# The second FFN of a diffusion layer on one Trainium2 core: where its first loads stand in the queue, where its operand forms are computed, and when a block's last turns are issued

## The chip, the cores and the metric

The kernel runs on one core of one Trainium2 chip. The metric is the time of one execution on the device in microseconds (us). The kernel before took 2631.93 us in the median of 3 runs (2630.71 to 2635.68). The profile shows one more execution of it.

## What is computed

The reference is one layer of a diffusion backbone: a half-step SwiGLU FFN on 256 context tokens and 256 latent tokens, a token mixer (attention heads and mLSTM heads), and a second half-step SwiGLU FFN on the latent tokens alone, all in fp32. The change touches only the second FFN:

```python
def adaln(x, g, mod, i):
    return rms_norm(x, g) * (1 + mod[:, i + 1, None, :]) + mod[:, i, None, :]

def half_step_ffn(x, mod, i, g, w_up, w_down):
    h = adaln(x, g, mod, i)
    a, b = jnp.split(h @ w_up, 2, axis=-1)
    return x + 0.5 * mod[:, i + 2, None, :] * ((jax.nn.silu(a) * b) @ w_down)

    ...
    xl = half_step_ffn(xl, mod_l, 6, g_norm[l, 2], w_ffn2_up[l], w_ffn2_down[l])
    ...
    return rms_norm(xl, g_final)
```

Here x is 256 x 2048, w_up is 2048 x 11264 (two halves, a and b, of 5632 columns) and w_down is 5632 x 2048.

## The kernel before

**Split products.** Every fp32 factor is split into a high part, rounded to the matmul's input type (`hi`, ScalarE, line 123), and the remainder (`lo`, VectorE, line 124). One product is three matmuls, hi by hi, hi by lo, lo by hi (lines 145 to 147). A weight tile is 128 x 2048 fp32, 1 MB, and is split in two halves of 1024 columns. The halves go into a pool of four `hi` and four `lo` buffers, so the split of a half waits until TensorE has used up the half four places before it. Weights that are used as they come land in `raw`, a pool of three buffers; the next load into a buffer waits for the `lo` of the tile that it held.

**Blocks of columns.** The 5632 columns of the hidden layer are 11 blocks (numbers 0 to 10) of 512. Block 0 is worked out while the layer norm is still unfinished (`products`, `tail`); its last quarter (the two loads `in_w_up`, line 138) runs until the change's first place. Block 1 is the *plain block*: `up(1)` has eight steps, one 1 MB tile each and 24 matmuls of 128x512. Blocks 2 to 10 (`QUADS`) go through `quad(n)`, a scheme of seven half-size products in the manner of Strassen: 14 steps of one 1 MB tile and 12 matmuls each, into two PSUM accumulators X and Y. The left factors are quarters of h (`a11`, `a12`, `a22`) and four combinations of them, the *forms* `n1`, `s2`, `s4` and `s3`, each again as a high and a low part. They are computed once, by `token_forms`, with VectorE and ScalarE instructions. The right factors are combinations of weight tiles, and these are formed in SBUF: a tile of the *chain* is loaded, split, and then another weight tile is added to it by an accumulating DMA that GpSimd (POOL) issues (`accum`, line 726). There are two sets of two such tiles, `chain2c` and `chain2r`, and they change roles from block to block.

**The order of the work.** The program text sets it, and the tile framework then orders the instructions of each engine by its own estimate. First come three steps of `up(1)`, each followed by a step of `token_forms`; then quad 2 with the other five steps of `up(1)` and the first of `down0` between its steps; from then on each quad has four steps of the down product (24 matmuls each) between its 14 steps. Each engine takes its instructions in order, and so does the queue of SP, which issues most loads: an issue that waits for its buffer holds up all issues behind it.

**The two places of the change.** At the first, after block 0, the pools of the layer norm are closed and three things are put on the right side of SBUF in their place: the accumulator of the output `acc2` (128 x 2 x 2048), the four chain tiles and the forms. The first loads of the four chain tiles stand right behind this in the program (lines 1985 to 1988). `token_forms` takes one buffer of the `raw` pool for its two temporaries, from its first step until `s3` has been written, which waits for the sixth tile of `up(1)`. At the second place, the end of each quad, `c21` works out the second half of the gated values (`ca`, 128 tokens x 512 columns), and its *turn* is entered in a list: four 128x128 transposes on TensorE (line 2053) and two instructions that put the result into the hidden tiles `hid2h` and `hid2l`. A turn is issued when the clock that counts the steps has reached its entry; that of `c21` is entered with 2 steps to go.

## Time and profile before

| | |
|---|---|
| median of 3 runs | 2631.93 us |
| the profiled execution | 2630.98 us, its span 2629.3 us |
| TensorE busy | 2580.3 us, 98% of the span |
| VectorE busy | 2181.8 us, 83% |
| ScalarE busy | 1446.4 us, 55% |
| mean granted TensorE clock | 0.993 |
| second FFN from the plain block on | 1950.5 us to the end |

The page of the profile gives busy times over the whole span; the stage of the change is its last quarter. In the rows that follow, PE is TensorE, DVE is VectorE, ACT is ScalarE, SPq is SP's queue of DMA issues. A row of the timeline has the start, the duration, engine, line, operation, output and inputs by the program's names, the shape and the count; in square brackets stands how long the engine had been idle and what ended that. A row of the waits has the waiting engine and line, what it waited for, the sum in us, the number of waits and the longest.

### The profile page before, as it was taken

What the parts mean: (1) busy time and instruction counts of PE and PEld (TensorE: products, weight loads), DVE (VectorE), ACT (ScalarE), POOL (GpSimd) and SP (SyncE); (2) the same over time, 40 slices, a digit from 0 to 9 for tenths busy, and PEclk for the clock granted to TensorE, in tenths of its full rate; (3) what the DMA queues carried; (4) which work ended last, traced back from release to release, by engine and by line L of the source; (5) the groups of instructions that cost most, each with busy time, mean ns of one, the idle gap of its engine ahead of it and who ended that gap; (6) DMA issues with size and microseconds to landing.
All of it is one profiled execution on the core that took longest, in us unless ns stands there. A gap on an engine that the chain in (4) does not pass through costs nothing. (4 is left out here: it accounts for less than half of the span.)

```text
span 2629.3 us, 33786 instructions
## 1 busy us (share of the span) xinstructions
PE 2580.3 (98%) x12646; PEld 2141.9 (81%) x12646; DVE 2181.8 (83%) x2842; ACT 1446.4 (55%) x1862; POOL 221.2 (8%) x275
## 2 busy tenths in 40 slices
PE   8999999999999999999999999999989999999998
PEld 5788888888888878888889889878887877887787
DVE  7788888878888778888886889788987888888888
ACT  4454544454444465444454467566565766666664
POOL 0000010100010100000110000120000000000001
PEclk8999999999999999999999999999999999999999
DMA  9989999999999988889986877677667889999996
GB/s 390 356 211 267 282 267 283 253 271 283 278 268 282 262 238 235 226 217 231 230 236 267 313 260 260 229 252 283 235 233 208 262 257 266 268 269 260 268 273 196
DMA packets 127795, 685.20 MB, mean 261 GB/s; under 512 B 14216, under 2 KB 16776, under 8 KB 65040
## 3 DMA queue, kind: packets, MB, share of 16 engines
q1 hardware_dynamic: 98256, 491.15, 49.8%
q0 software_dynamic: 29376, 191.90, 37.0%
q8 instruction: 99, 1.62, 0.2%
q14 instruction: 64, 0.52, 0.1%
HBM read 665.11 MB, written 17.89 MB: 260 GB/s over the span
## 5 line engine op out<-in xcount | busy, mean ns | idle before, releaser
L123 ACT ACTIVATE hi<-raw 128x1024 fp32r<-128x1024 f32 (+2 forms) x488 | 504.3, 1040 | 410.3 <-PE mm L147 255.0
L124 DVE TENSOR_TENSOR lo<-raw,hi 128x1024 fp32r<-128x1024 f32 (+2 forms) x476 | 569.7, 1209 | 159.6 <-ACT hi L123 139.6
L145 PE MATMUL mm<-hi,hhi 128*128 128x512 f32 (+3 forms) x1024 | 393.8, 385 | 0.0
L146 PE MATMUL mm<-lo,hhi 128*128 128x512 f32 (+3 forms) x1024 | 386.9, 378 | 0.0
L147 PE MATMUL mm<-hi,hlo 128*128 128x512 f32 (+3 forms) x1024 | 386.9, 378 | 0.0
L123 ACT ACTIVATE hi<-chain 128x1024 fp32r<-128x1024 f32 x240 | 253.1, 1059 | 239.4 <-PE mm L147 131.8
L124 DVE TENSOR_TENSOR lo<-chain,hi 128x1024 fp32r<-128x1024 f32 x240 | 290.2, 1222 | 77.3 <-ACT hi L123 76.0
L203 DVE SCALAR_TENSOR_TENSOR junk<-sraw,cBh 128x1024 fp8e5<-128x1024 f32 x192 | 234.5, 1221 | 25.4 <-DMA sraw<-in_w_mt 23.1
L147 PEld LDWEIGHTS mm<-hi,hlo 128*128 128x128 f32 x1024 | 192.5, 188 | 33.8
L145 PEld LDWEIGHTS mm<-hi,hhi 128*128 128x128 f32 x1024 | 192.6, 188 | 31.1
L146 PEld LDWEIGHTS mm<-lo,hhi 128*128 128x128 f32 x1024 | 192.8, 188 | 30.6
L124 DVE TENSOR_TENSOR lo<-chain2c,hi 128x1024 fp32r<-128x1024 f32 x112 | 135.5, 1223 | 43.5 <-ACT hi L123 39.4
L123 ACT ACTIVATE hi<-chain2c 128x1024 fp32r<-128x1024 f32 x112 | 117.0, 1058 | 81.6 <-PE mm L147 40.0
L124 DVE TENSOR_TENSOR lo<-chain2r,hi 128x1024 fp32r<-128x1024 f32 x104 | 125.9, 1223 | 41.0 <-ACT hi L123 37.2
L123 ACT ACTIVATE hi<-chain2r 128x1024 fp32r<-128x1024 f32 x104 | 108.8, 1058 | 71.1 <-PE mm L147 30.7
L146 PE MATMUL mm<-lo,hid2h 128*128 128x512 f32 x352 | 137.4, 391 | 0.7 <-DVE lo L124 0.7
L147 PE MATMUL mm<-hi,hid2l 128*128 128x512 f32 x352 | 136.9, 389 | 0.0
L145 PE MATMUL mm<-hi,hid2h 128*128 128x512 f32 x352 | 135.8, 389 | 0.0
L203 DVE SCALAR_TENSOR_TENSOR sr<-sr,cBl 128x1024 f32<-128x1024 f32 x85 | 102.6, 1218 | 15.2 <-DMA sr<-in_w_mt 15.0
L726 POOL DMA_DIRECT2D chain<-in_w_up1b x60 | 53.0, 884 | 723.9 <-DVE lo L124 697.0
L145 PE MATMUL mm<-hhi,hi 128*128 128x512 f32 (+1 forms) x288 | 101.2, 351 | 0.0
L146 PE MATMUL mm<-hlo,hi 128*128 128x512 f32 (+1 forms) x288 | 98.9, 343 | 0.0
(513 smaller groups left out, 5848.7 us busy)
## 6 DMA issues: line engine op xcount, KB each, us to landing
raw<-in_w_dn SPq DMA_DIRECT2D x70, 1024.0 KB, 9.7
chain<-in_w_up1b POOLq DMA_DIRECT2D x60, 1024.0 KB, 10.8
sraw<-in_w_mt SPq DMA_DIRECT2D x96, 512.0 KB, 8.5
sr<-in_w_mt SPq DMA_DIRECT2D x82, 512.0 KB, 5.2
raw<-in_w_up1b SPq DMA_DIRECT2D x40, 1024.0 KB, 8.2
mraw<-in_w_m SPq DMA_DIRECT2D x32, 1024.0 KB, 7.5
chain<-in_w_dn POOLq DMA_DIRECT2D x30, 1024.0 KB, 8.5
chain2c<-in_w_up2b POOLq DMA_DIRECT2D x28, 1024.0 KB, 12.3
```

Of the source, the lines that this page charges most:

```text
L123: scalar[0].activation(hi, src, AF.Copy)
L124: vector[0].tensor_tensor(lo, src, hi.bitcast(F32), op=ALU.subtract)
L145: tensor[0].matmul(out_ap, sh, mh, start=first, stop=False, skip_group_check=skip)
L146: tensor[0].matmul(out_ap, sh, ml, start=False, stop=False, skip_group_check=skip)
L147: tensor[0].matmul(out_ap, sl, mh, start=False, stop=last, skip_group_check=skip)
L203: ins = nc.vector.scalar_tensor_tensor(junk() if junk else raw, raw, 1.0, cB[s], op0=ALU.mult, op1=ALU.mult, accum_out=mT[:, i, s, kt, h : ...
L726: accum = lambda dst, src: nc.gpsimd.dma_start(dst, src, accum_op=ALU.add)
```

## The change

The change has four parts, all in the second FFN.

1. The first loads of the chain tiles move in the program: those of `chain2c` behind the second step of the plain block (the load of its second tile), those of `chain2r` behind step 1 of quad 2.
2. The two temporaries of `token_forms` are no longer a `raw` buffer but columns 1024 to 2047 of `acc2`; the gate's values of the plain block (`sab`) stand in columns 0 to 511 of `acc2`. `down0` writes these columns later.
3. The turn of `c21` is entered with 4 steps to go in place of 2.
4. `sab` of block 0 moves to a pool that is closed after block 0, and the last block's temporary takes a `ca` buffer.

```diff
         def sab_tile():
-            return f2.tile([P, CB], F32, tag="sab", name="sab")
+            return scratch[-1].tile([P, CB], F32, tag="sab", name="sab", bufs=2)
...
-        for q in range(2):
-            nc.sync.dma_start(sets[0][q], part(QUADS[0], 0, q))
-        for q in range(2):
-            nc.sync.dma_start(sets[1][q], part(QUADS[0], 1, 2 + q))
+        def first_tiles(ab, c, tiles):
+            for q in range(2):
+                nc.sync.dma_start(tiles[q], part(QUADS[0], ab, c + q))
...
-            raw = raw_tile()
-            vs = [raw[:, x * 1024 : (x + 1) * 1024].rearrange("p (k c) -> p k c", k=8) for x in range(2)]
+            vs = [acc2[:, x, 1024:].rearrange("p (k c) -> p k c", k=8) for x in range(2)]
...
                 mul(g["a"], g["a"], g["y"])
-                turn.append((clock[0] + 2, n, 1, g["a"], -1.0))
+                turn.append((clock[0] + 4, n, 1, g["a"], -1.0))
...
-                                sab.append(sab_tile())
+                                sab.append(acc2[:, t, :CB])
...
-        for _ in range(3):
+        for n in range(3):
             unit()
+            if n == 1:
+                first_tiles(0, 0, sets[0])
             steps(forms)
         for n in QUADS:
...
                 clock[0] += 1
                 turned()
+                if n == QUADS[0] and step == 1:
+                    first_tiles(1, 2, sets[1])
                 if step % 2:
...
-                    y = sab_tile()
+                    y = ca_tile()
```

What this makes of the order, at three places. First the queue of SP, from the last quarter of block 0 (`in_w_up`) on; `raw<-in_w_up2b` of line 138 are the tiles of the plain block, those of line 2121 (now 2119) the first tiles of quad 2 that are used as they come. Before:

```order
L138 DMA raw<-in_w_up 128x2048 x2
L138 DMA raw<-in_w_up2b 128x2048
L1986 DMA chain2c_16100<-in_w_up2b 128x2048
L1986 DMA chain2c_16101<-in_w_up2b 128x2048
L1988 DMA chain2r_16102<-in_w_up2b 128x2048
L1988 DMA chain2r_16103<-in_w_up2b 128x2048
L138 DMA raw<-in_w_up2b 128x2048 x4
L2121 DMA raw<-in_w_up2b 128x2048 x2
```

And with the change:

```order
L138 DMA raw<-in_w_up 128x2048 x2
L138 DMA raw<-in_w_up2b 128x2048 x3
L1987 DMA chain2c_16100<-in_w_up2b 128x2048
L1987 DMA chain2c_16101<-in_w_up2b 128x2048
L1987 DMA chain2r_16102<-in_w_up2b 128x2048
L1987 DMA chain2r_16103<-in_w_up2b 128x2048
L138 DMA raw<-in_w_up2b 128x2048 x2
L2119 DMA raw<-in_w_up2b 128x2048 x2
```

Two tiles of the plain block now stand ahead of the four chain tiles.

Second, VectorE where block 0 ends and the forms begin; `raw` on the left of an arrow is the temporary of the forms, `lo<-raw,hi` is the split of a weight tile. Before:

```order
L1935 TENSOR_TENSOR hid2l<-sab,hid2h 128x256
L2013 TENSOR_TENSOR raw<-raw,h2lo 128x1024
L1999 TENSOR_TENSOR raw<-h2hi 128x1024
L1999 TENSOR_TENSOR raw<-raw,h2lo 128x1024
L2013 TENSOR_TENSOR raw<-raw,h2lo 128x1024
L1999 TENSOR_TENSOR n1f<-raw,n1f 128x1024
L1999 TENSOR_TENSOR raw<-raw,h2lo 128x1024
L2000 SCALAR_TENSOR_TENSOR raw<-raw,h2hi 128x1024
L1999 TENSOR_TENSOR raw<-raw,h2lo 128x1024
L1999 TENSOR_TENSOR s2f<-raw,s2f 128x1024
L2000 SCALAR_TENSOR_TENSOR raw<-raw,h2hi 128x1024
L124 TENSOR_TENSOR lo<-raw,hi 128x1024 x4
```

And with the change, where the temporary is `acc`:

```order
L1935 TENSOR_TENSOR hid2l<-sab,hid2h 128x256
L2011 TENSOR_TENSOR acc_16099<-acc_16099,h2lo 128x1024
L124 TENSOR_TENSOR lo<-raw,hi 128x1024
L1998 TENSOR_TENSOR acc_16099<-acc_16099,h2lo 128x1024
L124 TENSOR_TENSOR lo<-raw,hi 128x1024
L1998 TENSOR_TENSOR acc_16099<-h2hi 128x1024
L1998 TENSOR_TENSOR n1f<-acc_16099,n1f 128x1024
L124 TENSOR_TENSOR lo<-raw,hi 128x1024
L1999 SCALAR_TENSOR_TENSOR acc_16099<-acc_16099,h2hi 128x1024
L124 TENSOR_TENSOR lo<-chain2c_16100,hi 128x1024
L1998 TENSOR_TENSOR acc_16099<-acc_16099,h2lo 128x1024
L124 TENSOR_TENSOR lo<-chain2c_16100,hi 128x1024
```

The instructions of the forms no longer stand in one run ahead of four splits; a split stands behind each one or two of them. One more split (of the second plain tile) stands a few rows higher.

Third, TensorE at the start of a quad, where the turn of the quad before it stands (`tr<-ident,ca`). X is the first product, Y the second. Before, ahead of the last three matmuls of X:

```order
L146 MATMUL X<-lo,h2hi 128x512
L147 MATMUL X<-hi,h2lo 128x512
L2053 MATMUL tr<-ident,ca 128x128 x4
L145 MATMUL X<-hi,h2hi 128x512
L146 MATMUL X<-lo,h2hi 128x512
L147 MATMUL X<-hi,h2lo 128x512
L145 MATMUL Y<-hi,h2hi 128x512
```

And with the change, behind the twelfth of the 24 matmuls of Y:

```order
L145 MATMUL Y<-hi,h2hi 128x512
L146 MATMUL Y<-lo,h2hi 128x512
L147 MATMUL Y<-hi,h2lo 128x512
L2051 MATMUL tr<-ident,ca 128x128 x4
L145 MATMUL Y<-hi,h2hi 128x512
L146 MATMUL Y<-lo,h2hi 128x512
```

In quads 4 to 10 the turn moves back by 15 matmuls; the two instructions that take its result move with it, on both engines behind three more splits.

## The prediction

> **What bounds the kernel now.** First the page, for the engine that is busy longest:

> ```profile
> span 2629.3 us, 33786 instructions
> PE 2580.3 (98%) x12646; PEld 2141.9 (81%) x12646; DVE 2181.8 (83%) x2842; ACT 1446.4 (55%) x1862; POOL 221.2 (8%) x275
> ```

> TensorE (PE) is busy 98% of the span and the change takes no matmul away. So it can win only where TensorE stands idle, or runs at a lower granted clock, in the second FFN. The table by stages, from the plain block on, shows where that is (stretch, length, busy time and count of TensorE, its weight loads, VectorE, ScalarE and GpSimd, granted clock, DMA share, GB/s):

> ```profile
> 1950.70:1956.10 5.40, 5.40 (x24) 4.13 (x22) 5.34 (x7) 0.43 (x2) 0.00 (x0) 1.00 1.02 431
> 1956.10:1971.40 15.30, 5.91 (x15) 4.21 (x15) 13.93 (x12) 5.96 (x7) 0.00 (x0) 0.67 0.54 218
> 2001.20:2008.80 7.60, 5.06 (x15) 3.73 (x15) 5.73 (x6) 4.60 (x6) 0.00 (x0) 0.78 0.64 233
> 2124.40:2132.40 8.00, 6.28 (x20) 4.47 (x19) 5.78 (x6) 5.04 (x6) 0.14 (x1) 0.79 0.85 330
> 2132.40:2570.40 438.00, 430.12 (x1905) 350.79 (x1904) 377.14 (x350) 291.59 (x308) 36.45 (x42) 1.00 0.91 264
> ```

> Two holes lie in the plain block: A (15.3 us, 5.91 busy, clock 0.67) and B (7.6 us, 5.06 busy, clock 0.78). A third lies at the end of quad 3, and the 438 us behind it lose 7.9. TensorE's timeline has the idle times of A and B in brackets, between the first matmul of the plain block and the first of `n1` (product 3 of quad 2):

> ```profile
> 1950.49 0.40 PE L145 MATMUL mm<-hi,h2hi 128*128 128x512 f32 x1
> 1950.72 0.40 PE L146 MATMUL mm<-lo,h2hi 128*128 128x512 f32 x1
> ...
> 1964.02 1.22 PE L145 MATMUL mm<-hi,h2hi 128*128 128x512 f32 x2 [7.91 <-ACT hi L123]
> 1966.73 0.80 PE L146 MATMUL mm<-lo,h2hi 128*128 128x512 f32 x1 [1.49 <-DVE lo L124]
> ...
> 2003.06 0.50 PE L145 MATMUL mm<-hi,h2hi 128*128 128x512 f32 x1 [1.78 <-ACT hi L123]
> 2004.32 0.50 PE L146 MATMUL mm<-lo,h2hi 128*128 128x512 f32 x1 [0.76 <-DVE lo L124]
> ...
> 2011.30 0.39 PE L145 MATMUL Y<-hi,n1f 128*128 128x512 f32 x1
> ```

> Both end with a split. What the splits waited for stands on ScalarE, VectorE and SP's queue:

> ```profile
> 1945.58 0.80 SPq L1986 DMA_DIRECT2D chain2c<-in_w_up2b  x2
> 1947.60 0.92 SPq L138 DMA_DIRECT2D raw<-in_w_up2b  x2
> 1951.10 1.22 DVE L1999 TENSOR_TENSOR raw<-h2hi 128x1024 f32<-128x1024 f32 x1
> 1961.97 1.06 ACT L2006 ACTIVATE s2f<-raw 128x1024 fp32r<-128x1024 f32 x1 [4.82 <-DVE raw L1999]
> 1962.93 1.04 ACT L123 ACTIVATE hi<-raw 128x1024 fp32r<-128x1024 f32 x1
> 1997.10 2.60 SPq L138 DMA_DIRECT2D raw<-in_w_up2b  x2
> 2001.95 1.06 ACT L123 ACTIVATE hi<-raw 128x1024 fp32r<-128x1024 f32 x1 [4.24 <-DMA raw<-in_w_up2b]
> 2012.37 1.23 DVE L1999 TENSOR_TENSOR h2lo<-raw,h2hi 128x1024 fp32r<-128x1024 f32 x1 [0.64 <-ACT h2hi L2006]
> ```

> Hole A: plain tiles 2 and 3 are issued at 1947.60, behind the four chain tiles, and ScalarE takes tile 2 only at 1962.93, behind the copy of `s2` for which it had stood 4.82 us. Hole B: the load for the sixth plain tile is issued at 1997.10 and waited for; one of three `raw` buffers is the forms' until 2012.37, so two carry the stream.

> The waits of SP (1925 to 1990) and TensorE (2009 to 2580), by sum, count and longest:

> ```profile
> SPq L1986 <- DVE sab L1946: 12.0, 1, 12.0
> ...
> PE tr L2053 <- DVE ca L2071: 4.6, 6, 0.8
> PE Y L146 <- DVE lo L124: 2.9, 4, 0.8
> PE Y L145 <- ACT hi L123: 1.2, 2, 1.0
> ```

> SP stood 12.0 us, to 1945.58, before the first chain tile's issue, with the plain tiles behind it. And six times TensorE waits 0.8 us at the turn of `c21` for its product on VectorE (`ca`, L2071).

> **What the holes cost.** Idle: 7.91 + 1.49 + 1.78 + 0.76 = 11.9 us. Half clock: in A, (1 - 0.67) x 15.3 = 5.05 us lost at half rate means 10.1 us at it; idle were 1.49 and, from 1961 to 1964, some 3.2 of these, so 5.4 us of work cost 2.7 more; in B (1 - 0.78) x 7.6 = 1.7. Sum 16.3. End to end: 192 matmuls (six plain tiles of 24, four quad steps of 12) from 1950.49 to 2011.30 at 0.23 us, the step of the first two rows, are 44.2 of 60.8 us: 16.6 lost. I take 16.5.

> The idle 2.54 us of B was followed by a lower clock, so was 1.73 us at quad 3 (0.97 + 0.76), but not 1.04 us at quad 7:

> ```profile
> 2126.64 0.51 PE L145 MATMUL Y<-hi,h2hi 128*128 128x512 f32 x1 [0.97 <-ACT hi L123]
> 2127.90 0.67 PE L146 MATMUL Y<-lo,h2hi 128*128 128x512 f32 x1 [0.76 <-DVE lo L124]
> ...
> 2378.43 0.49 PE L145 MATMUL Y<-hi,h2hi 128*128 128x512 f32 x1 [0.28 <-ACT hi L123]
> 2379.69 0.50 PE L146 MATMUL Y<-lo,h2hi 128*128 128x512 f32 x1 [0.76 <-DVE lo L124]
> ...
> 2376.00:2384.00 8.00, 6.88 (x28) 4.86 (x27) 5.59 (x6) 5.96 (x6) 0.00 (x0) 1.00 0.96 375
> ```

> [...]

> **The change, part by part.**

> *The queue of SP.* Ahead of the chain tiles only buffers bind. The second and third plain tile take those of block 0's last two tiles, whose `lo` end at the first two rows:

> ```profile
> 1937.42 1.23 DVE L124 TENSOR_TENSOR lo<-raw,hi 128x1024 fp32r<-128x1024 f32 x1
> 1942.16 1.22 DVE L124 TENSOR_TENSOR lo<-raw,hi 128x1024 fp32r<-128x1024 f32 x1
> 1965.46 4.62 DVE L124 TENSOR_TENSOR lo<-raw,hi 128x1024 fp32r<-128x1024 f32 x4
> ...
> raw<-in_w_up2b SPq DMA_DIRECT2D x26, 1024.0 KB, 6.7
> ```

> So they are issued at 1938.7 and 1943.4 and land, at the median of 6.7 us, at 1945.4 and 1950.1. TensorE needs them at 1950.49 + 24 x 0.23 = 1956.0 and at 1961.5: covered by 10.6 and 11.4 us. The chain tiles are still issued at 1945.58, since their release (L1946) does not move; four tiles of 1.05 MB at the 431 GB/s of the first row are there by 1955.8, needed at 1967: covered by 11 us. The one POOL queue (accumulations) is fed by the chain's splits and moves forward with them.

> *The forms in `acc2`.* Three buffers carry the plain tiles all along. Tile 4 goes out behind the chain tiles and is needed at 1972.6; the sixth, late in B, goes out once tile 5 is split, near 1978, and is needed near 1990 (1972.6 + 72 matmuls). Hole B closes. Whether `acc2` waits for what lay under it the trace does not show: between 0 and the 12.0 us that SP waited for the neighbouring tiles. I take 0, because that wait ended at 1945.58 and the first form starts at 1951.10. VectorE is what is left: by the order it has 11 form instructions and 8 splits between the last `sab` (1951.1) and the split of the fourth plain tile, 19 x 1.14 us (the run of four in 4.62 us: 1.13 from start to start, 1.22 the last) and 0.34 for `hid2l`: done at 1973.1, needed at 1950.49 + 96 x 0.23 + 0.23 = 1972.8. I leave 0.5 us idle; bounds 0 and 3.1 (1.4 us idle, the middle of 1.04 and 1.73, and half clock behind it, 1.7).

> *The turn, 15 matmuls later.* 15 x 0.23 = 3.4 us covers the 0.8 us six times, 4.6 in all. But the next wait is close. At `n1` the chain tile's accumulation lands late; the rows of quads 5 and 8:

> ```profile
> 2211.85 2.01 ACT L123 ACTIVATE hi<-chain2r 128x1024 fp32r<-128x1024 f32 x2 [2.78 <-DMA chain2r<-in_w_up2b]
> 2218.58 1.22 DVE L124 TENSOR_TENSOR lo<-raw,hi 128x1024 fp32r<-128x1024 f32 x1
> 2220.02 0.39 PE L146 MATMUL mm<-lo,hid2h 128*128 128x512 f32 x1
> ...
> 2401.14 1.06 ACT L123 ACTIVATE hi<-chain2c 128x1024 fp32r<-128x1024 f32 x1 [3.72 <-DMA chain2c<-in_w_up2b]
> 2409.13 0.50 PE L146 MATMUL mm<-lo,hid2h 128*128 128x512 f32 x1 [0.33 <-DVE lo L124]
> ```

> From landing to TensorE runs an unbroken chain of `hi`, three `lo`, one tile addition (2.29 us) and one more `lo`. It hangs on the landing, not on the turn. In quad 5 it ends at 2218.58 + 1.22 = 2219.80, 0.2 us ahead of the matmul that reads it (2220.02); in quad 8 TensorE already waits 0.33. So of the 0.8 us won at a turn, 0.2 stay in a quad like 5 and nothing in one like 8: the wait only moves. I take 0.2 for quads 5, 6, 9 and 10 and 0 for 7 and 8, 0.8 together, and keep 0 and 4.6 as bounds.

> *Pools.* `sab` and `y` change addresses only; the `ca` buffers that `y` takes were last read by quad 10's turns, three down steps earlier. Nothing.

> **Sum.** 2630.98 - 16.5 + 0.5 - 0.8 = 2614.2 us for the profiled execution. The median of the runs is 0.95 above that execution: 2615.1.

> **Rivals.**

> *VectorE keeps a part of hole A (0.10).* If a split waits for a buffer just as a form is ready, the in-order chain slips; 3 us of slip and its half clock give 2615.1 + 2.5 + 1.7 = 2619.3. For: VectorE is full from 1951 to 1973, its slack 0.3 us. Against: every split in my count finds its `hi` by then.

> *DMA gives it back (0.06).* TensorE would be 16 us ahead and quads 3 and 4 wait for weights instead: if the hole at quad 3 grows by 13 to 16 us, 2628 to 2631. For: DMA share 0.91 over the quads. Against: 0.54 and 0.64 in A and B; the loads move forward too. [...]

> *Slower: half clock in every quad (0.04).* TensorE comes 0.8 us earlier to the tile that quad's last product takes, and the loads of the down product, earlier too, share the DMA engines with the accumulation into it. Today that wait (the rows of L145 and L146 on Y) is 1.73 us in quad 3, 1.04 in quad 7 and 1.3 in all the other quads together (2.9 + 1.2 less these two). If the accumulations land over 1.5 us later, it passes the point between 1.04 and 1.73 us in each of quads 4 to 10: 7 x (1.7 idle + 1.7 for half clock) = 23.8, less the 2.4 that stand there today, less 16 won: 2632 + 5 = 2637. For: quad 3 shows it once, DMA share 0.91. Against: the accumulation starts from a split that TensorE paces itself, behind the turn, so it moves with TensorE.

> *The change does not reach the queue:* excluded, since SP's order shows both tiles ahead.

> **How the numbers follow.** Forecast 0.80, VectorE 0.10, DMA 0.06, slower 0.04. Low end: no residue, all 4.6 us of the turns, and the 1.73 us idle at quad 3 gone by a new phase: 2615.1 - 0.5 - 3.8 - 1.7 = 2609.1; with a part of its half clock gone too, 2608. High end: residue 3.1, nothing from the turns, half clock once more: 2615.1 + 2.6 + 0.8 + 1.7 = 2620.2; with the VectorE rival's 2619 inside I close at 2620.5. About 0.2% (5.3 us) is what a measurement of this kernel tells from no change: faster 0.90, same 0.06, slower 0.04.

> **What would show it.** Right: TensorE without a break from 1950.5 to the first `n1` matmul, now near 1995, clock 1.00 throughout; plain tile 2 issued near 1938.7; no wait at the turn, and 0.5 to 1.1 us of new wait at `n1` in each quad from 5 on. Wrong: an idle time over 1.4 us near 1971 to 1976, a hole at quad 3 that has grown by several us, or half clock in the quads.

## The result, and the profile after

The changed kernel took 2615.26 us in the median of 4 runs (2613.28 to 2618.03), the kernel before 2631.32 us beside it (4 runs, 2629.84 to 2635.68): a ratio of 0.9937, with a 95% interval of 0.9919 to 0.9956. In a second set of runs the same kernel gave 0.9942 (0.9925 to 0.9960). The forecast was 2615.1 us, range 2608 to 2620.5. The profiled execution took 2613.28 us, 17.70 less than that of before.

The head of the page after:

```profile
span 2611.5 us, 33782 instructions
PE 2577.5 (99%) x12646; PEld 2139.1 (82%) x12646; DVE 2179.6 (83%) x2842; ACT 1445.9 (55%) x1862; POOL 221.5 (8%) x275
```

The table by stages of the changed kernel (same columns as before): the plain block's start, the stretch where hole A was, that of hole B 17 us earlier than before, the end of quad 3, and the 438 us behind it:

```profile
1940.00:1956.10 16.10, 16.10 (x115) 15.18 (x115) 14.12 (x19) 9.34 (x14) 0.00 (x0) 1.00 0.88 347
1956.10:1971.40 15.30, 15.30 (x70) 12.65 (x69) 15.30 (x15) 9.38 (x10) 0.96 (x1) 1.00 0.89 301
1984.20:1994.30 10.10, 10.10 (x47) 8.35 (x46) 9.48 (x9) 6.46 (x8) 0.00 (x0) 1.00 0.77 300
2107.40:2115.40 8.00, 8.00 (x37) 6.61 (x36) 7.87 (x9) 6.79 (x7) 1.70 (x2) 1.00 1.03 403
2115.40:2553.40 438.00, 430.36 (x1891) 347.89 (x1890) 373.36 (x347) 286.47 (x305) 34.87 (x41) 1.00 0.91 263
```

TensorE is busy in every microsecond of the first four stretches and the clock is 1.00 in all of them: A and B are gone, and so is the hole at quad 3, on which only the low end of the forecast's range had counted. VectorE is full in the second (15.30 of 15.30) and TensorE does not wait for it, by a narrow margin. The split of the fourth plain tile and the matmuls that read it:

```profile
1972.05 2.35 DVE L124 TENSOR_TENSOR lo<-raw,hi 128x1024 fp32r<-128x1024 f32 x2
```
```profile
1972.52 1.07 PE L145 MATMUL mm<-hi,h2hi 128*128 128x512 f32 x4
1973.43 0.39 PE L146 MATMUL mm<-lo,h2hi 128*128 128x512 f32 x1
```

The first `lo` is ready at 1972.05 + 1.22 = 1973.27, 0.2 us later than forecast (1973.1) and later than the second matmul of the tile would have started. But in the order of the changed kernel four hi by hi matmuls stand ahead of the first that reads `lo`, and that one starts at 1973.43. In the last stretch 7.6 us are lost, hardly less than the 7.9 of before.

SP's queue, and TensorE's first matmul of `n1`:

```profile
1938.94 5.05 SPq L138 DMA_DIRECT2D raw<-in_w_up2b  x2
1945.85 0.81 SPq L1987 DMA_DIRECT2D chain2c<-in_w_up2b  x2
```
```profile
1994.30 0.39 PE L145 MATMUL Y<-hi,n1f 128*128 128x512 f32 x1
```

Plain tile 2 goes out at 1938.94 (forecast 1938.7), the chain tiles at 1945.85 as before, and `n1` begins at 1994.30 (forecast: near 1995). What TensorE waits for from there on (1990 to 2590), and two of these waits in quads 4 and 5:

```profile
PE Y L146 <- DVE lo L124: 4.7, 7, 0.8
PE mm L146 <- DVE lo L124: 1.6, 5, 0.3
PE Y L145 <- ACT hi L123: 0.6, 2, 0.4
```
```profile
2171.61 0.50 PE L146 MATMUL Y<-lo,h2hi 128*128 128x512 f32 x1 [0.76 <-DVE lo L124]
...
2195.61 0.50 PE L146 MATMUL Y<-lo,n1f 128*128 128x512 f32 x1 [0.75 <-DVE lo L124]
...
2201.22 0.50 PE L146 MATMUL mm<-lo,hid2h 128*128 128x512 f32 x1 [0.33 <-DVE lo L124]
```

No row of the turn is left. In its place TensorE waits at `n1` and the down step behind it (`Y<-lo,n1f`, `mm<-lo,hid2h`), and at the last product.

**Where the 17.7 us went.** Stretches of TensorE between the same matmuls in the two traces, before and after: first matmul of the plain block to the first of `n1` in quad 2, 60.81 and 43.56 (17.25 won); from there to `n1` of quad 3, 72.74 in both; to `n1` of quad 4, 64.87 and 61.05 (3.82 won); from there to the last product of quad 10, 415.86 and 418.98 (3.12 lost). What lies ahead of and behind these takes 0.25 of it. The forecast had 16.0, 0, 0 and 0.8.

### The profile page after: what moved, and what is told of

It is laid out like the page before. It is cut to its first block, busy times and chain, and to the rows that moved or that the text cites. A ratio compares the mean times of both kernels' runs of the same rounds, so it can differ in the third digit from the quotient of the medians.

```text
span 2611.5 us, 33782 instructions
## 1 busy us (share of the span) xinstructions
PE 2577.5 (99%) x12646; PEld 2139.1 (82%) x12646; DVE 2179.6 (83%) x2842; ACT 1445.9 (55%) x1862; POOL 221.5 (8%) x275
## 3 DMA queue, kind: packets, MB, share of 16 engines
q0 software_dynamic: 29376, 191.90, 37.5%
## 4 chain that ended last, share of the span: by engine, by line
PE 78%; DMA 9%; DVE 6%; issue 4%; ACT 2%; POOL 1%; POOLq 0%; ACTq 0%; SPq 0%; DVEq 0%
PE mm L146 20%; PE mm L147 19%; PE mm L145 19%; DMA chain2r<-in_w_up2b 3%; DVE lo L124 3%; PE mm L83 3%; DMA chain2c<-in_w_up2b 2%; PE Y L146 1%; PE Y L147 1%; PE Y L145 1%; PE tr L146 1%; PE tr L147 1%; PE tr L145 1%; PE tr L83 1%; PE X L147 1%
## 5 line engine op out<-in xcount | busy, mean ns | idle before, releaser
L123 ACT ACTIVATE hi<-raw 128x1024 fp32r<-128x1024 f32 (+2 forms) x488 | 504.3, 1040 | 410.4 <-PE mm L147 253.1
L124 DVE TENSOR_TENSOR lo<-raw,hi 128x1024 fp32r<-128x1024 f32 (+2 forms) x476 | 568.3, 1206 | 145.9 <-ACT hi L123 126.8
L145 PE MATMUL mm<-hi,hhi 128*128 128x512 f32 (+3 forms) x1024 | 394.4, 385 | 0.0
L146 PE MATMUL mm<-lo,hhi 128*128 128x512 f32 (+3 forms) x1024 | 387.4, 378 | 0.0
L123 ACT ACTIVATE hi<-chain 128x1024 fp32r<-128x1024 f32 x240 | 253.0, 1059 | 234.9 <-PE mm L147 130.7
L124 DVE TENSOR_TENSOR lo<-chain,hi 128x1024 fp32r<-128x1024 f32 x240 | 289.9, 1221 | 79.2 <-ACT hi L123 77.9
L145 PEld LDWEIGHTS mm<-hi,hhi 128*128 128x128 f32 x1024 | 193.0, 188 | 31.3
L146 PEld LDWEIGHTS mm<-lo,hhi 128*128 128x128 f32 x1024 | 193.0, 189 | 30.8
L124 DVE TENSOR_TENSOR lo<-chain2c,hi 128x1024 fp32r<-128x1024 f32 x112 | 135.6, 1222 | 39.6 <-ACT hi L123 36.0
L124 DVE TENSOR_TENSOR lo<-chain2r,hi 128x1024 fp32r<-128x1024 f32 x104 | 125.8, 1222 | 42.0 <-ACT hi L123 38.7
L123 ACT ACTIVATE hi<-chain2c 128x1024 fp32r<-128x1024 f32 x112 | 117.3, 1059 | 77.7 <-PE mm L147 37.1
L123 ACT ACTIVATE hi<-chain2r 128x1024 fp32r<-128x1024 f32 x104 | 108.7, 1058 | 73.2 <-PE mm L147 34.1
L146 PE MATMUL mm<-lo,hid2h 128*128 128x512 f32 x352 | 137.8, 392 | 1.8 <-DVE lo L124 1.6
L145 PE MATMUL mm<-hi,hid2h 128*128 128x512 f32 x352 | 135.8, 389 | 0.0
L145 PE MATMUL mm<-hhi,hi 128*128 128x512 f32 (+1 forms) x288 | 101.1, 351 | 0.0
L146 PE MATMUL mm<-hlo,hi 128*128 128x512 f32 (+1 forms) x288 | 98.9, 344 | 0.0
## 6 DMA issues: line engine op xcount, KB each, us to landing
raw<-in_w_dn SPq DMA_DIRECT2D x70, 1024.0 KB, 10.2
chain<-in_w_up1b POOLq DMA_DIRECT2D x60, 1024.0 KB, 10.7
raw<-in_w_up1b SPq DMA_DIRECT2D x40, 1024.0 KB, 8.6
mraw<-in_w_m SPq DMA_DIRECT2D x32, 1024.0 KB, 7.5
chain<-in_w_dn POOLq DMA_DIRECT2D x30, 1024.0 KB, 9.0
chain2c<-in_w_up2b POOLq DMA_DIRECT2D x28, 1024.0 KB, 12.2
```

The source lines that it names most:

```text
L123: scalar[0].activation(hi, src, AF.Copy)
L124: vector[0].tensor_tensor(lo, src, hi.bitcast(F32), op=ALU.subtract)
L145: tensor[0].matmul(out_ap, sh, mh, start=first, stop=False, skip_group_check=skip)
L146: tensor[0].matmul(out_ap, sh, ml, start=False, stop=False, skip_group_check=skip)
```

## The experiments

The runs of the kernel before beside each set of runs have medians from 2628 to 2631 us, so kernels of different sets are compared by their ratios to before.

**The two edits of the plain block, and the turn, each alone on the kernel before.** `forms`:

```diff
-            raw = raw_tile()
-            vs = [raw[:, x * 1024 : (x + 1) * 1024].rearrange("p (k c) -> p k c", k=8) for x in range(2)]
+            vs = [acc2[:, x, 1024:].rearrange("p (k c) -> p k c", k=8) for x in range(2)]
```

> The kernel before with one edit alone: the two temporaries of the forms stand in acc2 (columns 1024 to 2047) instead of a raw buffer. Theory of the prediction (the queue's order closes hole A, the buffer closes hole B): A stays, B goes, 2631.3 - 4.2 = 2627.1 us, SP still stands 12.0 us ahead of the first chain tile with two plain tiles behind it. Rival (the raw buffer held by the forms is the cause of both holes, since with three free buffers the second and third plain tile go out ahead of the chain tiles in SP's queue anyhow): both holes close, 17.25 us by the two traces (60.81 us from the first matmul of the plain block to n1 before, 43.56 after), and the turn's six waits of 0.8 us stay: 2614.1 us, or 2610 to 2612 if the hole at quad 3 (3.9 us by the same comparison) closes by the new phase and not by the turn.

Measured: 2611.15 us, 0.9931 (0.9916 to 0.9946). The rival was right. The stretch of the plain block took 43.58 us, as with the whole change, and no wait is left in it. In the order of its instructions this kernel differs from the change only in the turn: with the third `raw` buffer free, the tile framework itself puts two plain tiles ahead of the chain tiles, wherever their loads stand in the program. This one edit carries the whole win.

`queue`:

```diff
+            if n == 1:
+                first_tiles(0, 0, sets[0])
...
+                if n == QUADS[0] and step == 1:
+                    first_tiles(1, 2, sets[1])
```

> The kernel before with one edit alone: the first loads of the chain tiles stand later in the program, as in the change; the forms keep their raw buffer. Theory of the prediction: hole A goes (9.4 us idle and its half clock, 12.3 in all), B stays: 2619.0 us. Rival (the buffer, not the program's place of the loads): the forms hold one of three raw buffers, so the chain2c loads still go out ahead of plain tiles 2 and 3, and only the two chain2r issues (2 x 0.5 us) move behind them; plain tile 2 goes out near 1946.6 in place of 1947.6: 2629.5 to 2631.5 us.

Measured: 2617.59 us, 0.9956 (0.9942 to 0.9971). Against the 2627.98 us beside it 10.4 us are won; the prediction's theory had 12.3, the rival at most 1.8. The rival fell, though its picture of the queue was right. SP's longest wait, ScalarE around the second plain tile, and TensorE's idle times in the plain block:

```profile
SPq L1987 <- DVE sab L1946: 11.8, 1, 11.8
```
```profile
1954.16 1.06 ACT L2005 ACTIVATE n1f<-raw 128x1024 fp32r<-128x1024 f32 x1 [4.46 <-DVE raw L1998]
1955.12 3.88 ACT L123 ACTIVATE hi<-raw 128x1024 fp32r<-128x1024 f32 x4
...
1962.18 1.06 ACT L2005 ACTIVATE s2f<-raw 128x1024 fp32r<-128x1024 f32 x1 [0.85 <-DVE raw L1998]
```
```profile
1956.21 0.73 PE L145 MATMUL mm<-hi,h2hi 128*128 128x512 f32 x2 [2.03 <-ACT hi L123]
1957.66 0.51 PE L146 MATMUL mm<-lo,h2hi 128*128 128x512 f32 x1 [0.72 <-DVE lo L124]
...
1992.37 0.73 PE L145 MATMUL mm<-hi,h2hi 128*128 128x512 f32 x2 [1.55 <-ACT hi L123]
1993.63 0.80 PE L146 MATMUL mm<-lo,h2hi 128*128 128x512 f32 x1 [0.53 <-DVE lo L124]
```

SP still stands 11.8 us. But plain tile 2 has two chain tiles ahead of it and not four: by the landings in the trace it took 8.8 us (1944.57 to 1953.34), before 12.5 (1947.60 to 1960.14). And the order that results puts its split ahead of the copy of `s2`, where before it stood behind. The rival had priced the earlier issue (1 us) and forgotten both. Hole A shrinks from 9.4 us idle to 2.75, hole B stays; the stretch took 51.62 us, 9.2 won of 17.25, so hole A did not close whole either.

`turn_only`:

```diff
-                turn.append((clock[0] + 2, n, 1, g["a"], -1.0))
+                turn.append((clock[0] + 4, n, 1, g["a"], -1.0))
```

> The kernel before with one edit alone: the turn of c21 is entered with 4 steps to go. Theory of the prediction: the six waits of 0.8 us go and come back at n1 but for 0.8 us in all: 2630.5 us (2626.7 if they all go). Rival: TensorE, ahead by what a turn took (0.93 us by the marks of the two traces), runs into both accumulations of each quad, at n1 and at the last product, and each new wait costs its idle and a restart of some 0.4 us; in the trace of the change the quads 4 to 10 took 3.1 us longer than before: 2634.4 us if that is the turn's doing and not the phase's.

Measured: 2628.55 us against 2627.98, 1.0000 (0.9989 to 1.0011), so within 2.9 us of nothing. The repeat of the change, beside which it is to be read:

> The changed kernel once more, beside the kernel before on the chip of this call, to set the turn's worth against the run of the forms' edit alone (which measured 0.9931 of before, and whose order differs from that of the change only in the turn). Theory of the prediction, that 0.8 us of the turn's six waits stay: 0.9928 of before. Rival, that the turn costs the quads 3.1 us net: 0.9943.

Measured: 2612.33 us, 0.9942 (0.9925 to 0.9960); the interval holds both values. The traces say more. TensorE's idle times over 0.1 us from quad 3 on, by place, and its time from `n1` of quad 2 to the last product of quad 10:

| kernel | turn | n1 and the step behind it | last product | us, n1 to last product |
|---|---|---|---|---|
| before (2 steps) | 4.6 | 0.7 | 4.1 | 553.5 |
| forms (2 steps) | 4.6 | 0.5 | 5.6 | 555.1 |
| queue (2 steps) | 5.0 | 1.4 | 2.5 | 552.4 |
| changed (4 steps) | 0 | 2.7 | 4.4 | 552.8 |
| changed, repeat (4 steps) | 0 | 4.1 | 1.6 | 550.8 |
| turn_only (4 steps) | 0 | 4.8 | 2.0 | 550.8 |

Of the waits of TensorE from 1990 us on, the two longest rows of `forms` and then of `turn_only`, which has no row of the turn (0.8 us of its second row are hole B's):

```profile
PE tr L2052 <- DVE ca L2070: 4.6, 6, 0.8
PE Y L146 <- DVE lo L124: 3.8, 5, 0.8
```
```profile
PE Y L146 <- DVE lo L124: 3.2, 5, 0.8
PE mm L146 <- DVE lo L124: 3.0, 8, 0.8
```

The wait does move to `n1`: 0.5 to 1.4 us there with the turn at 2 steps, 2.7 to 4.8 with 4. The means of the last column are 553.7 and 551.5, 2.2 us for the early turn with a scatter of 2 to 3. From quad 4 on nothing is won (415.9, 417.6 and 416.1 against 419.0, 416.2 and 417.1); all of it lies between `n1` of quads 3 and 4 (64.87, 64.74 and 63.62 against 61.05, 61.90 and 61.04). There the issues of the four accumulations that follow one another stand at the same places, 19.9 to 20.0 us behind `n1` for the fourth, but the fourth lands 20.4 to 21.6 us later with the turn at 2 steps and 17.1 to 19.6 with 4. So the turn does not cost the quads 3.1 us, as the rival had it. The timed runs do not show a win: 1.0000 alone, and the change (0.9937, 0.9942) is not below `forms` (0.9931), which has the turn at 2 steps.

**Do the landings of the accumulations pace the quads?** `no_accumulation` leaves the accumulations out, so its result is not the layer's, and their traffic goes with them:

```diff
-                return lambda q: accum(chain_[q], part(n, ab, c + q))
+                return None
...
-                (s4, third, "Y", False, lambda q: accum(ra[q], part(n, 1, q)), p35),
+                (s4, third, "Y", False, None, p35),
```

> The changed kernel without the accumulations of the quads: 54 tiles are not added (the right factors are then the single tiles), which leaves out 56.6 MB of traffic and every wait for a landing of POOL's queue. It bounds what these landings cost in all. Theory (n1 and a22 wait for landings): no wait at n1 or a22, the quads without idle time, 2615 - 9 = 2606 us. Rival (VectorE's chain of three splits and a tile addition ends last by itself): n1 keeps 0.3 us of wait in each quad, 2609 to 2611 us.

Measured: 2598.45 us, 0.9888 (0.9870 to 0.9906). TensorE over 420 us of quads:

```profile
2120.00:2540.00 420.00, 420.00 (x1880) 347.47 (x1879) 372.72 (x345) 289.47 (x303) 0.00 (x0) 1.00 0.46 170
```

Not one wait is left, and the DMA share is 0.46 in place of 0.91. So `n1` and the last product wait for the accumulations or for the traffic that these bring (the run takes both away), and VectorE's chain behind them is fast enough by itself. In all they cost 14 us (2612.33 less 2598.45), more than the idle times show (5.6 to 7.1), since each wait also has a restart (0.35 us on top of 0.76 in the rows of quad 4 above) and the repeat of the change has one stretch of half clock (such a stretch, 3.41 us at 0.50 at quad 3 of the kernel before, costs 1.7 us).

The landings themselves, of the four accumulations that follow one another in quad 5 of the changed kernel:

```
issue 2203.85  2207.23  2209.95  2213.16
land  2211.68  2218.56  2226.04  2233.44
```

They are issued 3 us apart and land 7 us apart, one after the other: the first takes 7.8 us, the fourth 20.3. The last product reads the third and the fourth.

`unit_before_n1`, more time ahead of the first landing:

```diff
-            behind = {0: 2, 1: 1, 2: 1, 3: 1, 4: 1, 5: 1, 6: 1} if n == QUADS[0] else {1: 1, 2: 1, 4: 1, 5: 1}
+            behind = {0: 2, 1: 1, 2: 1, 3: 1, 4: 1, 5: 1, 6: 1} if n == QUADS[0] else {0: 1, 1: 1, 4: 1, 5: 1}
```

> The kernel after, with the down step that stands behind n1 in quads 3 to 10 moved ahead, between a11 and a12: 24 matmuls (24 x 0.227 = 5.4 us) more between the split of the chain tile that starts the accumulation for n1 and the matmul that reads it. Theory (the distance of 72 matmuls, 16.3 us, is too short for the accumulation and the chain of splits behind it): the waits at n1 in quads 4 to 10 go, 4.9 us by the marks of the two traces: 2610.4 us. Rival 1 (the DMA engines are full, 0.91 busy, and the wait only moves to the last product or to s3): 2613 to 2617 us, with the waits of a22 grown by as much as those of n1 shrink. Rival 2 (without a down step behind n1 VectorE's two additions of 2.29 us and four splits come late for s4): a wait of 1 us or more at s4 in each of 8 quads, 2620 us or more.

Measured: 2654.33 us, 1.0096 (1.0079 to 1.0113). Its waits of TensorE, and ScalarE's for the down tiles:

```profile
PE mm L145 <- ACT hi L123: 16.4, 7, 2.7
PE mm L146 <- DVE lo L124: 5.0, 7, 0.8
...
PE Y L145 <- ACT cy L2083: 4.8, 7, 0.7
```
```profile
ACT hi L123 <- DMA raw<-in_w_dn: 40.0, 8, 5.9
```

No wait stands at `n1` any more. In quads 4 to 10 the second landing for it comes 8.2 to 10.9 us ahead of `n1`, in the change 0.1 to 1.7 us behind its start. Its issue stands 8.9 to 11.9 us farther ahead; the moved matmuls are 5.4 of these and the new waits the rest, so by this estimate the distance alone would have been enough. But two down tiles and the two plain tiles between them now follow one another in three `raw` buffers, and the second down tile comes 1.9 to 2.7 us late in seven quads; `s4`, without a down step ahead of it, also waits 0.7 us for the copy of Y (`cy`). Rival 2 had the sign and the wrong place.

`halves`, each accumulation as two of 128 x 1024:

```diff
+            def halves(dst, src):
+                for w in (slice(0, 1024), slice(1024, 2048)):
+                    accum(dst[:, w], src[:, w])
```

> The changed kernel, with each accumulation into a chain tile of the quads issued as two of 128 x 1024 columns, each behind the split of its own half. Theory (the landing of the accumulation ends last at n1 and at the last product, and the first half is needed 24 x 0.227 = 5.4 us ahead of nothing else): the first half lands some microseconds earlier and the waits at n1 and a22 go, 6.9 us idle and some 0.4 us of restart for each of 14: 2615 - 9 = 2606 us at best, 2609 if the second halves still land late. Rival 1 (the 16 DMA engines serve both halves and the loads in turn, so that both land when the whole did): 2614 to 2616 us. Rival 2 (twice the descriptors make the accumulations slower): 2618 us or more, with longer times from issue to landing of the second halves.

Measured: 2631.12 us, 1.0011 (0.9999 to 1.0023), the whole win gone. Its waits, and the last product's first matmuls in quad 9 with the stretch around them:

```profile
PE Y L145 <- ACT hi L123: 11.8, 7, 2.2
PE Y L146 <- DVE lo L124: 5.3, 7, 0.8
```
```profile
2503.55 0.50 PE L145 MATMUL Y<-hi,h2hi 128*128 128x512 f32 x1 [2.23 <-ACT hi L123]
2504.81 0.52 PE L146 MATMUL Y<-lo,h2hi 128*128 128x512 f32 x1 [0.76 <-DVE lo L124]
```
```profile
2499.00:2510.00 11.00, 8.01 (x28) 5.89 (x27) 7.70 (x8) 5.73 (x6) 2.59 (x3) 0.84 0.84 298
```

`n1` is free, but the last product waits 2.0 to 3.0 us in each of seven quads, with half clock behind it every time: the granted clock is 0.84 in the 11 us above and 0.97 over 420 us of quads (2120 to 2540), in the change 1.00. The halves of the last two tiles land at 2223.58, 2228.59, 2233.63 and 2238.63 in quad 5: 10 us a tile in place of 7.4 (those of the two tiles before land 2.5 to 2.9 us apart, so not every tile is slower). They are packets of 4 KB (37152 on POOL's queue, before 29376) beside loads in packets of 8 KB. The queue with the smaller packets gets less here: in the slices of 0.5 us of the quads (2130 to 2540, by the ends of the packets) in which both queues move over 10 KB, POOL's moves 132 GB/s beside SP's 159 in the change and 99 beside 213 here. In slices that it has to itself it moves 201 and 194, so smaller packets alone cost it little there. The next runs turn this round.

`halves_n1`. Its text speaks of the first and the fifth product's accumulations; the kernel cut only the first's (those with `ab` 1):

```diff
+                put = halves if ab else accum
+                return lambda q: put(chain_[q], part(n, ab, c + q))
```

> The changed kernel with only those accumulations in halves that n1 and s2 wait for (the first and the fifth product's, chained), the one of s4 whole as before. In the run with all accumulations in halves n1 never waited, but the last product waited 1.2 to 2.2 us for its hi and 0.76 for its lo in each quad. Theory A (POOL's queue works off one accumulation after the other, 7.4 us each for a whole tile by the landings of the changed kernel, 2211.68, 2218.56, 2226.04, 2233.44 us; the second product group needs the last of four, and halves of 4 KB packets only get a smaller share beside loads of 8 KB packets, 10 us a tile by the landings of the halved run): the last product is again the one that pays, its wait between that of the changed kernel and that of the halved run, n1 stays free: 2616 to 2628 us. Theory B (the halves were late because the accumulations of s4 were cut): a22 back to the changed kernel's waits, n1 free: 2608 us.

Measured: 2619.60 us, 0.9964 (0.9951 to 0.9977). Both theories had `n1` free, and it is `n1` that pays: its waits and those of the step behind it sum to 10.8 us, up to 1.72 in quad 6, while the last product waits 2.3. In `halves` it had been free because TensorE came to it later, held up at the last product before: in quads 4 to 10 the last half for `n1` is issued 11.0 to 12.2 us ahead of `n1` there, 8.1 to 9.6 here, and lands 9.7 to 12.2 us after its issue there, 11.9 to 12.8 here.

`loads_4k` and `loads_4k_all`, the accumulations whole and SP's loads in halves (TensorE's, VectorE's and ScalarE's instructions in the same order as in the change):

```diff
+            def loads(dst, src):
+                for w in (slice(0, 1024), slice(1024, 2048)):
+                    nc.sync.dma_start(dst[:, w], src[:, w])
...
-                    nc.sync.dma_start(ra[q], part(n + 1, 0, q))
+                    loads(ra[q], part(n + 1, 0, q))
...
-                        wt = load_split(I["w_dn2"][m, cb])
+                        raw = raw_tile()
+                        for w in (slice(0, 1024), slice(1024, 2048)):
+                            nc.sync.dma_start(raw[:, w], I["w_dn2"][m, cb][:, w])
+                        wt = split(raw)
```

(The last hunk is in `loads_4k_all` alone.)

> The changed kernel with the four plain loads of the next quad's chain tiles issued as two of 128 x 1024 columns each (packets of 4 KB in place of 8 KB); accumulations whole. The order on TensorE, VectorE and ScalarE is the same. Theory (beside other transfers a queue's share goes by packets, so smaller packets of the loads leave more to the accumulations): the last of the four accumulations lands 1 to 3 us earlier, the waits at a22 go, 3 to 4 us of 2612.3: 2608 us. Rival (the share goes by bytes; the halved accumulations were late for another reason): no change, 2611 to 2614 us. Rival 2 (the chain tiles of the next quad come late for its first product): slower by 2 us and more in each quad, 2630 us.

> As loads_4k, and the weight tiles of the down product in the quads in halves too: all of SP's loads of the quads but the first and second plain tile in packets of 4 KB. Theory (share by packets): the accumulations for n1, beside which the down tiles are loaded, gain as well; both waits go, 6 to 9 us of 2612.3: 2604 to 2607 us, with accumulations of 6 us in place of 7.4. Rival (bytes): no change, 2611 to 2614 us. Rival 2: down tiles arrive late, TensorE waits at their splits: 2620 us or more.

Measured: 2608.43 us, 0.9923 (0.9910 to 0.9935), and 2601.36 us, 0.9898 (0.9884 to 0.9912). The waits of TensorE in the one, and in the other:

```profile
PE Y L146 <- DVE lo L124: 4.9, 7, 0.8
PE mm L146 <- DVE lo L124: 2.2, 7, 0.3
PE Y L145 <- ACT hi L123: 0.6, 1, 0.6
```
```profile
PE mm L146 <- DVE lo L124: 1.2, 5, 0.3
```

`loads_4k_all` is 1.0% below the kernel before and 0.4% below the change; of the runs that compute the whole layer only `loads_4k_turn2` below equals it. The gain of `loads_4k` on the change lies within the intervals. In `loads_4k` the last product never waits: all that is left stands at `n1` and the step behind it. In `loads_4k_all` 1.2 us are left. The mean times from issue to landing in quads 4 to 10, of the two accumulations for `n1` and of the four in a row: changed 8.8, 13.4 | 8.0, 11.4, 15.9, 19.9; `loads_4k` 10.2, 14.7 | 8.2, 10.6, 14.9, 18.2; `loads_4k_all` 10.0, 13.3 | 8.0, 10.7, 15.1, 18.3. Against the change the last of the four gains 1.6 us, as the theory has it, but against its repeat, where it takes 18.7, only 0.5; the last product never waits in either version. The shares move as the theory has it: where both queues move data, POOL's gets 145 GB/s beside 136 in `loads_4k_all`. The accumulations for `n1` gain nothing, so what freed `n1` in `loads_4k_all` is not shown; a down tile whose first half can be split before its second has landed would do it too.

`loads_2k_all` (the same in quarters) and `loads_4k_turn2` (`loads_4k_all` with the turn at 2 steps):

> As loads_4k_all, with the same loads of the quads issued as four of 128 x 512 columns (packets of 2 KB). Theory (share by packets): the accumulations get a still larger share, the last of four lands 1 us or more earlier and the remaining 1.4 us at n1 goes: 2599 to 2601 us, near the 2598.5 us without any accumulation. Rival (packets of 2 KB move less per time, or SP's four issues per tile hold up the queue): the loads come late, TensorE waits at splits of down tiles or at the first product: 2605 us or more.

> The version with SP's loads in packets of 4 KB (2601.4 us, only 0.1 to 0.3 us of wait at n1 left in six quads), with the turn of c21 back to 2 steps. Theory (the prediction's: the early turn's 0.8 us was eaten by late landings, so where these are gone it keeps its worth): the six waits of 0.78 us come back with 0.15 us each of restart, less up to 1.4 us that stands at n1 now: 2601.4 + 4.2 to 5.6 = 2605.6 to 2607 us. Rival (the turn is worth nothing, since what it saves is lost at other places than the landings): 2600 to 2602.5 us.

Measured: 2606.40 us, 0.9905 (0.9889 to 0.9922), and 2604.05 us, 0.9898 (0.9883 to 0.9913). Quarters do not help further: POOL's queue now gets 158 GB/s beside 106, but the last accumulation takes 18.1 us, hardly less, and `n1` with the step behind it waits 7.1 us again. So the share follows the packets and the landings do not follow the share; why was not found. Of the second kernel the waits:

```profile
PE tr L2051 <- DVE ca L2069: 3.6, 5, 0.8
PE Y L146 <- DVE lo L124: 1.5, 2, 0.8
```

In its trace the way from `n1` to the last product takes 547.3 us against 542.3, 5 us for the early turn where no landing is late, as expected (4.2 to 5.6). But the profiled execution, 2606.22 us, is the slowest of its four, and the ratios of the timed runs are equal, with intervals of 3.9 us to either side. The turn's worth in this version stays open.

## Why the prediction was right, step by step

- **The holes are TensorE's whole loss in the plain block**: right, and short by 0.6 us. 60.81 - 43.56 = 17.25 were lost, not 16.6: the step between matmuls is 43.56 / 192 = 0.227 us, and two digits (0.23) were too few for 192 of them.
- **SP's order closes A, the `acc2` columns close B**: this step was wrong as an attribution. The forms' edit alone closes both (43.58 us); the moved loads alone take 9.2 of A; on top of the forms' edit they add nothing, since the order is then the same. The sum holds both holes and does not depend on which edit closes them, so it came out right all the same. The prediction read the order with all edits in it and gave each edit its own share; building each edit alone would have shown it.
- **`acc2` waits for nothing, VectorE leaves 0.5 us**: 0 and 0. VectorE was as late as counted (1973.27 for 1973.1). The count missed TensorE's order: it let the second matmul of the fourth plain tile read `lo`, near 1972.8, and three more hi by hi matmuls stand ahead of that one. 0.16 us were left.
- **The turn's 4.6 us come back at `n1` but for 0.8**: right as a mechanism (0.5 to 1.4 us at `n1` become 2.7 to 4.8) and, from `n1` of quad 4 on, within the scatter in size. The sign that it named, 0.5 to 1.1 us of new wait in each quad from 5 on, came in two of six quads of the profiled execution (1.1 in quad 5, 0.5 in quad 10, 0 to 0.3 in the others). The step did not see quad 3, where 1.7 to 3.8 us go with the early turn; why its landings come in time then was not found.
- **Pools: nothing.** `forms`, without that edit, is no slower.
- **The sum** of 2614.2 met 2613.28 because three terms that it had at 16.0, 0 and +0.8 were 17.25, +3.8 and -3.1. The first is a size, with the 0.5 us of VectorE in it; the second goes with the turn; the third lies within the scatter, for the changed kernel and its repeat differ by 2.8 us there (418.98 and 416.16). That the last two nearly cancel is luck, and so is the hit to within 1 us.
- **The rivals.** VectorE's slip did not come, by the 0.16 us above, nor did the return through DMA. The slower one, half clock in every quad once landings are 1.5 us later, did not come either, but `halves` shows that it is real and that the change stands close to it: seven half clocks, and 18 us by the ratios (1.0011 against 0.9942).

## What to carry to other kernels

A buffer that a side task holds can cost more than the wait that the profile puts to it: here one of three buffers also decided the order of a queue, so try each edit alone before sharing out the win. The wait removed ahead of a transfer that landed just in time came back at the landing here (0.5 to 1.4 us at `n1` became 2.7 to 4.8); look first at what lands late there, and whether transfers that run beside it can be made to give way (`loads_4k_all`, 0.4% below the change). Idle times that add up to 1.6 us or more within 3.4 us are worth removing for the half clock that followed them here in 22 of 23 windows of the grid below, some 1.7 us for a stretch of 3.41; whether it followed depended on where they fell (half clock behind 1.72 us at quad 3 before, none behind 1.84 us there in `forms`).

## What the runs showed of the hardware

```profile
2106.50 0.51 PE L145 MATMUL Y<-hi,h2hi 128*128 128x512 f32 x1 [1.08 <-ACT hi L123]
2107.76 0.50 PE L146 MATMUL Y<-lo,h2hi 128*128 128x512 f32 x1 [0.76 <-DVE lo L124]
```
```profile
2104.00:2112.00 8.00, 6.08 (x25) 4.17 (x24) 5.52 (x6) 5.93 (x6) 0.00 (x0) 1.00 0.81 313
```

**The accumulating transfers landed one after the other**, 6.9 to 7.5 us apart for 1 MB beside other loads (quad 5 of the change, above). By itself POOL's queue moved 201 GB/s in the quads of the change, SP's 348; there a packet of 8 KB took 0.67 us of a DMA engine in the mean when it accumulated and 0.33 when it was a plain load. Where both queues moved data, the share went with the size of their packets: 99 GB/s for the accumulations beside 213 for the loads with 4 KB beside 8 KB, 132 beside 159 with 8 KB on both, 145 beside 136 with most loads in 4 KB, 158 beside 106 with most loads in 2 KB.

**A matmul that had waited cost more than its wait.** In the rows of quad 4 above it runs 0.50 us, where others run 0.39, and the next starts 0.34 us later (2171.95), where others follow after 0.23. With the 0.76 us of idle time TensorE loses 1.1 us, which is why the stretches lose more than the idle times sum to.
